# A two-layer decoder trunk: first pieces fetched first, norm squares on VectorE, matmuls in runs of two, three heads in flight

## The chip, the cores and the metric

The kernel runs on one core of a Trainium2 chip. A core has TensorE (matmuls; in the profile PE, with its weight loads as PEld), VectorE (DVE), ScalarE (ACT), GpSimd (POOL) and SyncE (SP, which here only issues transfers), an on-chip memory of 128 partitions (SBUF), and a small accumulator memory that matmuls write to (PSUM). Sixteen DMA engines move data from and to the chip's main memory. The metric is the device time of one execution in microseconds, as the median over several executions.

## The reference

Input x is 256 tokens of 2048 features, in float32. Two layers follow each other. Layer 0 mixes with a chunked gMLP (u, v) beside a gated linear recurrence, HGRN2 (q, f, i, g); layer 1 mixes with a forgetting attention of 16 heads. Each layer ends with a gated MLP that has a short convolution between its up-projection and its activation. Every part begins with an RMS norm and ends with a residual:

```python
def rms_norm(x, gain):
    xf = x.astype(jnp.float32)
    y = xf * lax.rsqrt(jnp.mean(xf * xf, axis=-1, keepdims=True) + RMS_EPS)
    return (y * gain.astype(jnp.float32)).astype(x.dtype)
...
for l in range(DEPTH):
    h = rms_norm(x, mix_norm[l])
    h = mixer_ab(h, ...) if l % 2 == 0 else mixer_c(h, ...)
    x = x + h
    h = rms_norm(x, ffn_norm[l])
    x = x + conv_ffn(h, ffn_w_up[l], ffn_conv_w[l], ffn_conv_b[l], ffn_w_down[l])
```

The projections hold nearly all of the arithmetic: six of 2048 x 1024 and one of 2048 x 2048 in layer 0's mixer, four of 2048 x 2048 (and a small one) and one of 2048 x 2048 in layer 1's, and in each MLP one of 2048 x 11264 and one of 5632 x 2048.

## The kernel before, in words

Features lie on partitions: x is held as 16 tiles (k-tiles) of 128 features by 256 tokens. A float32 product is made of three products of a narrower type: each operand is cut into a high part (a copy by ScalarE) and the rest (a subtraction by VectorE). `weights` (L129 to L142) does this for a chunk of weights: it has SP fetch the chunk into `w`, ScalarE make `wh` (L139) and VectorE `wl` (L141). The pool holds four `w` and three each of `wh` and `wl`; in the MLPs a second pool takes turns with it.

`project` (L144) makes one output tile of 128 features: 16 k-tiles (11 in the down projections) in two chunks. Each k-tile takes a pair of matmuls: `wh` against 512 columns, the high and the low part of the activations beside each other (L155), and `wl` against the 256 columns of the high part (L158). The argument `run` says how many `wh` matmuls stand in a row before their `wl` matmuls follow. Before the change it is 1 for f, q, g, u, w_cf and w_cg, 4 for w_abo and w_co, 2 for up and 3 for down in layer 0, 8 for up and 6 for down in layer 1.

`project_tok` (L164) makes tokens by features, 512 features at a time, for v, i and the attention's q, k, v. Each k-tile takes six matmuls 512 wide: L177, L178, L179 for each half of the tokens. For v's first half (`feed=True`) it also makes the activations on the way: `feed_split` scales a k-tile of x by the norm weights (columns of `pp`) and cuts it (L204, L205), and `feed_square` squares it on ScalarE (L240) and adds the squares into `acc` on GpSimd (L241). The first four chunks hold one k-tile, all others two.

The factor 1/rms is not in the activations: `norm.finish` gets it from `acc` with a matmul against ones and some small operations (`R`, and `Rt` for the token layout), and it is multiplied in after the projections. In v this is done by `finish`, a generator in a queue. `tick`, called once per chunk, advances up to `depth[0]` generators of the queue to their next `yield`; the recurrence's heads (`hgrn`), the gMLP's `mix` and the attention's heads run in the same way between the projections' chunks. A planner orders each engine's instructions from this program; every engine then takes its own in that fixed order.

At the start, GpSimd fetches the first 100 columns of `pp` (norm weights, hgrn gammas and other gains), SP the first piece of x, ScalarE the other four pieces, and TensorE runs 12 warm-up matmuls on a tile of ones. In layer 0's mixer ScalarE's queue later fetches the constants: `cst`, the gMLP's spatial weights `wt`, the rest of `pp`, and a mask.

`hgrn` (one generator per head) makes decay products at seven levels (`E`), their score matmuls (`smk`), adds them into `st`, and applies the result to i's tokens. `wt` and `E` share one tag of two buffers; `st` and `s128` have two buffers.

Of the kernel before, what the change touches and what calls it, by code (L numbers as in the profile page):

```python
# [7 lines left out]
F32 = mybir.dt.float32  # L8
# [6 lines left out]
P = 128  # L15
S = 256
D = 2048
KT = D // P
NH = 8
# [2 lines left out]
HT = HID // P  # L22
GRP = 11
EPS = 1e-6
WARM = 12
LEVELS = (64, 32, 16, 8, 4, 2, 1)
NL = len(LEVELS)
MCOLS = 2 * (NL + 1) * P
# [3 lines left out]
C_CW = 100  # L32
# [12 lines left out]
def tile_trunk(ctx: ExitStack, tc: tile.TileContext, x, pp_d, cst_d, mlev_d, msk_d,  # L45
# [13 lines left out]
    def nm(base):  # L59
        count[0] += 1  # L60
        return f"{base}_{count[0]}"

    xT = []
    xload = []
    for c0, n in ((0, 2), (2, 2), (4, 4), (8, 4), (12, 4)):
        t = cp.tile([P, n, S], F32, tag=f"x{c0}", name=f"x{c0}")
        xload.append((t, c0, n))
        xT += [t[:, i] for i in range(n)]
    pp = cp.tile([P, NPP], F32, tag="pp", name="pp")
    cst = cp.tile([P, NK], F32, tag="cst", name="cst")  # L70
    ones = cp.tile([P, P], F32, tag="ones", name="ones")
    one1 = cp.tile([P, 1], F32, tag="one1", name="one1")

    nc.gpsimd.dma_start(pp[:, 0:C_CW], pp_d[:, 0:C_CW])
    V.memset(ones, 1.0)
    V.memset(one1, 1.0)
    ident = cst[:, K_ID:K_ID + P]
# [37 lines left out]
    depth = [2]  # L115

    SC.preload_act_table_set(LNEXP)
    for i, (t, c0, n) in enumerate(xload):
        (SC if i else nc.sync).dma_start(t, x[:, c0:c0 + n, :])
    warm = pm.tile([P, 512], F32, tag="pm", name="warm")  # L120
    for i in range(WARM):
        PE.matmul(warm[:, 0:P], ones, ones, start=True, stop=True)
# [1 line left out]
    def drain():  # L124
        while flight or queue:
            tick()
# [14 lines left out]
        V.tensor_tensor(wl, w, wh.bitcast(F32), ALU.subtract)  # L141
        return wh, wl  # L142

    def project(wsrc, acts, chunks=(8, 8), k0=0, run=1):  # L144
        ps = pm.tile([P, 512], F32, tag="pm", name=nm("pm"))
        nk = sum(chunks)
        done = 0
        for c in chunks:
            lo = (k0 + done) * P
            tick()  # L150
            wh, wl = weights(wsrc[:, lo:lo + c * P], c * P)
            for k1 in range(0, c, run):
                ks = range(k1, min(k1 + run, c))
                for k in ks:
                    PE.matmul(ps, wh[:, k * P:(k + 1) * P], acts[done + k],  # L155
                              start=done + k == 0, stop=False, skip_group_check=True)
                for k in ks:
                    PE.matmul(ps[:, S:2 * S], wl[:, k * P:(k + 1) * P], acts[done + k][:, 0:S],  # L158
                              start=False, stop=done + k == nk - 1, skip_group_check=True)
            done += c  # L160
        return ps

    def project_tok(wsrc, norm, feed=False):
        ps = [pm.tile([P, 512], F32, tag="pm", name=nm("pm")) for _ in range(2)]  # L164
        k = 0
        for c in ((1, 1, 1, 1) + (2,) * 6 if feed else (2,) * 8):
            if feed:
                for i in range(c):
                    norm.feed_split(k + i)
            tick()  # L170
            wh, wl = weights(wsrc[:, k * 512:(k + c) * 512], c * 512)
            for T in range(2):
                for i in range(c):
                    a = norm.a[k + i]
                    ah, al = a[:, T * P:(T + 1) * P], a[:, S + T * P:S + (T + 1) * P]
                    h, l = (t[:, i * 512:(i + 1) * 512] for t in (wh, wl))
                    PE.matmul(ps[T], ah, h, start=k + i == 0, stop=False)  # L177
                    PE.matmul(ps[T], ah, l, start=False, stop=False)  # L178
                    PE.matmul(ps[T], al, h, start=False, stop=k + i == KT - 1)  # L179
            if feed:  # L180
                for i in range(c):
                    norm.feed_square(k + i, nc.gpsimd)
            k += c
        return ps

# [3 lines left out]
        V.tensor_tensor(t, ps[:, 0:S], t, ALU.add)  # L189
        return t  # L190

    def project_norm(wsrc, acts, R, out=None, run=1):
        t = fold(project(wsrc, acts, run=run))
        if out is None:
            out = t
        V.tensor_tensor(out, t, R, ALU.mult)  # L196
        return out
# [72 lines left out]
    def mixer_ab(norm):  # L270
# [10 lines left out]
        gv, late = [], []  # L281

        def finish():
            yield
            late.extend(norm.finish(tok=True))
            yield
            for T in range(2):
                act(gv[0][:, T], gv[0][:, T], AF.Gelu, scale=late[1][:, T:T + 1])
# [14 lines left out]
        A = norm.a  # L303

        SC.dma_start(cst, cst_d)
        wt = hp.tile([P, 2, NH, P], F32, tag="QK", name="wt", bufs=2)
        SC.dma_start(wt[:, 0], spw_d)
        SC.dma_start(wt[:, 1], spb_d.partition_broadcast(P))
        SC.dma_start(pp[:, C_CW:NPP], pp_d[:, C_CW:NPP])
# [63 lines left out]
        for h in range(NH):  # L373
# [9 lines left out]
            lf.append(l)  # L383
            kq.append(t)
        yB = [None] * KT

        itoks = []

        def hgrn(h):
            l, t = lf[h], kq[h]  # L390
            d0 = (h % 4) * P
            SC.activation(l, l, AF.Identity, bias=lb[:, h:h + 1], scale=omlb[:, h:h + 1])
            st = hp.tile([P, 2, P], F32, tag="st", name=nm("st"), bufs=2)
            dg = bank()
            for T in range(2):
                PE.matmul(dg[:, T * P:(T + 1) * P], t[:, T], t[:, 3 - T], start=True, stop=True)  # L396
# [2 lines left out]
            yield  # L399

            V.tensor_tensor(t[:, 2:4], t[:, 2:4], view(l, P, (-P, 2), (1, P)), ALU.mult)
            E = hp.tile([P, NL, 2, P], F32, tag="QK", name=nm("E"), bufs=2)
            tot = l
            for li in reversed(range(NL)):
                n = LEVELS[li]
# [17 lines left out]
            for c0, c1 in ((0, 4), (4, NL)):  # L423
                sps = bank()
                for li in range(c0, c1):
                    PE.matmul(sps[:, (li - c0) * P:(li - c0 + 1) * P],  # L426
                              E[:, li, 0], E[:, li, 1], start=True, stop=True)
                if c0 == 0:
                    xps = bank()
                    PE.matmul(xps[:, 0:P], t[:, 0], t[:, 2], start=True, stop=True)  # L430
                    s128 = hp.tile([P, P], F32, tag="s128", name=nm("s128"), bufs=2)
                    SC.activation(s128, xps[:, 0:P], AF.Copy)
                V.tensor_tensor(smk[:, c0 * P:c1 * P], sps[:, 0:(c1 - c0) * P],
                                msk[:, c0 * P:c1 * P], ALU.mult)
                for li in range(c0, c1):
                    n = LEVELS[li]
                    sv = view(st[:, 1], 0, (2 * n, 64 // n), (n - P, 2), (1, n))
                    V.tensor_tensor(sv, sv, smk[:, li * P:(li + 1) * P].rearrange(
                        "p (b two n) -> p b two n", two=2, n=n), ALU.add)
# [59 lines left out]
        for h in range(NH):  # L499
# [10 lines left out]
            if gates and not (queue or flight):  # L510
                queue.extend(spatial(b, z) for b, z in todo)
                todo = []
        drain()

        nxt = Norm(C_FFN)
        ks = [yB[8 + h] for h in range(NH)] + [yB[h] for h in range(NH)]
        for m in range(KT):
            add_x(m, project(w_abo[m], ks, run=4))
            nxt.feed(m)
        es.close()  # L520
        return nxt
# [2 lines left out]
    def mixer_c(norm):  # L524
# [109 lines left out]
            todo = []  # L634
        nxt = Norm(C_FFN + KT)
        for m in range(KT):
            add_x(m, project(w_co[m], yB, run=4))
            nxt.feed(m)
        es.close()
        return nxt  # L640
# [2 lines left out]
    def ffn(l, norm, last):  # L643
        es = ExitStack()
        hp = es.enter_context(tc.tile_pool(name="fp", bufs=1))
        deep.update(pool=es.enter_context(tc.tile_pool(name="fw", bufs=1)), turn=0)
        A = norm.a
        R = norm.finish()
        nxt = None if last else Norm(C_MIX + KT)

        def conv(j):
            z = project_norm(w_up[l, j], A, R, run=(2, 8)[l])

            def w(i):
                c = C_CW + (l * 3 + i) * 2 * HT + j
                return pp[:, c:c + 1]

            cb = C_CB + l * 2 * HT + j
            c = hp.tile([P, S], F32, tag="conv", name=nm("conv"), bufs=4)
            SC.activation(c, z, AF.Identity, bias=pp[:, cb:cb + 1], scale=w(2))  # L660
            V.scalar_tensor_tensor(c[:, 1:], z[:, :S - 1], w(1), c[:, 1:], ALU.mult, ALU.add)  # L661
            V.scalar_tensor_tensor(c[:, 2:], z[:, :S - 2], w(0), c[:, 2:], ALU.mult, ALU.add)  # L662
            return c

        def up(g):
            hid = []
            for i in range(GRP):
                j = g * GRP + i
                a = conv(j)
                b = conv(HT + j)  # L670
                act(a, a, AF.Silu)
                V.tensor_tensor(a, a, b, ALU.mult)
                t = hp.tile([P, 512], F32R, tag="hid", name=nm("hid"), bufs=2 * GRP)
                split(t, a)
                hid.append(t)
            return hid

        def down(g, hid):
            for m in range(KT):
                add_x(m, project(w_dn[l, m], hid, chunks=(6, 5), k0=g * GRP, run=(3, 6)[l]))  # L680
                if g == HT // GRP - 1:
                    if last:
                        nc.sync.dma_start(out[:, m, :], xT[m])
                    else:
                        nxt.feed(m)

        hids = [up(0)]
        for g in range(HT // GRP):
            if g + 1 < HT // GRP:
                hids.append(up(g + 1))  # L690
            down(g, hids[g])
        deep["pool"] = None
        es.close()
        return nxt
# [85 lines left out]
```

## Time and profile before

| | us |
|---|---|
| median of 3 runs (2371.09 to 2371.52) | 2371.42 |
| the profiled execution's own time | 2372.19 |
| its span, first to last instruction | 2370.4 |
| mean granted clock of TensorE over the span | 0.998 |
| TensorE busy | 2360.5 |
| VectorE busy | 1754.6 |
| ScalarE busy | 1324.8 |
| GpSimd busy | 16.2 |
| bytes read from main memory | 435.24 MB |

The profile is one execution. Its times count from the first instruction. A group or timeline line gives the line of the kernel, the engine, the operation, and the tiles as out<-in; in a timeline line the start and the duration stand first, and in brackets how long the engine was idle before and what ended that. A window line gives, for each engine, its busy time in that stretch and the number of instructions that touch it, then the granted clock of TensorE, the share of time that the DMA engines were busy, and GB/s. Matmuls overlap, so the duration of one is longer than its share of the time.

### The profile page before, as it was taken

The page shows a single profiled execution, that of the slowest core. Times are in us where ns is not written, and L with a number is a line of the kernel's source. Part 1 is how long each engine was busy: PE and PEld are TensorE (multiplying, and loading weights), DVE is VectorE, ACT ScalarE, POOL GpSimd, SP SyncE. Part 2 cuts the span into 40 slices and gives each one's busy share as a digit, 9 for nine tenths or more (in the row PEclk, how much of TensorE's full clock was granted, in tenths as well). Part 3 has the DMA queues.
Part 4 walks back from the last instruction along what each step waited for, and adds up shares of the span by engine and source line. Part 5 has one row for each costly group of instructions (what it writes and reads, how often), then busy time and mean ns, then how long its engine had stood idle before and what let it go on. Part 6 is the DMA issues. An engine that isn't in the chain of part 4 may idle for free.

```text
span 2370.4 us, 35641 instructions
## 1 busy us (share of the span) xinstructions
PE 2360.5 (100%) x13118; PEld 2045.7 (86%) x13118; DVE 1754.6 (74%) x2969; ACT 1324.8 (56%) x2249; POOL 16.2 (1%) x20
## 2 busy tenths in 40 slices
PE   9999999999999999999999999999999999999999
PEld 7888888888888888888888888888888888888888
DVE  7778886878767867867766666767778767767765
ACT  6655665655555555556555455556555555555543
POOL 2000000000000000000000000000000000000000
PEclk9999999999999999999999999999999999999999
DMA  7554455655575566566656554557555575575565
GB/s 259 178 167 153 152 190 202 223 191 190 156 211 198 167 193 206 172 174 187 198 170 182 171 161 167 187 189 238 194 187 187 155 223 189 153 222 189 153 190 145
DMA packets 133727, 439.69 MB, mean 185 GB/s; under 512 B 14865, under 2 KB 16929, under 8 KB 133425
## 3 DMA queue, kind: packets, MB, share of 16 engines
q1 hardware_dynamic: 132224, 433.40, 58.2%
q10 hardware_dynamic: 1296, 3.97, 0.5%
q8 instruction: 104, 1.70, 0.3%
q14 instruction: 71, 0.57, 0.1%
q0 software_dynamic: 32, 0.05, 0.0%
HBM read 435.24 MB, written 2.11 MB: 185 GB/s over the span
## 4 chain that ended last, share of the span: by engine, by line
PE 97%; DVE 2%; ACT 1%; issue 0%; DMA 0%; ACTq 0%; DVEq 0%; POOLq 0%
PE pm L155 53%; PE pm L158 27%; PE pm L178 5%; PE pm L177 5%; PE pm L179 5%; DVE wl L141 1%; PE px L426 1%; PE px L599 0%; PE px L563 0%; PE px L570 0%; DMA pp<-in_pp 0%; PE px L594 0%; DVE a L205 0%; PE px L396 0%; ACT wh L139 0%
## 5 line engine op out<-in xcount | busy, mean ns | idle before, releaser
L141 DVE TENSOR_TENSOR wl<-w,wh 128x1024 fp32r<-128x1024 f32 (+3 forms) x900 | 1015.8, 1129 | 519.2 <-ACT wh L139 513.4
L139 ACT ACTIVATE wh<-w 128x1024 fp32r<-128x1024 f32 (+3 forms) x900 | 883.2, 982 | 904.4 <-PE pm L155 635.1
L155 PE MATMUL pm<-a,wh 128*128 128x512 f32 x3600 | 1074.7, 395 | 0.0
L158 PE MATMUL pm<-a,wl 128*128 128x256 f32 x3600 | 694.5, 281 | 0.0
L155 PEld LDWEIGHTS pm<-a,wh 128*128 128x128 f32 x3600 | 614.9, 189 | 79.4 <-DVE a L205 0.8
L158 PEld LDWEIGHTS pm<-a,wl 128*128 128x128 f32 x3600 | 604.6, 189 | 76.5 <-issue 0.2
L155 PE MATMUL pm<-hid,wh 128*128 128x512 f32 x1408 | 389.0, 394 | 0.0
L155 PEld LDWEIGHTS pm<-hid,wh 128*128 128x128 f32 x1408 | 239.3, 189 | 27.9
L158 PEld LDWEIGHTS pm<-hid,wl 128*128 128x128 f32 x1408 | 219.8, 189 | 33.6
L158 PE MATMUL pm<-hid,wl 128*128 128x256 f32 x1408 | 228.9, 281 | 0.0
L177 PE MATMUL pm<-wh,a 128*128 128x512 f32 x512 | 203.8, 399 | 3.0 <-ACT wh L139 3.0
L178 PE MATMUL pm<-wl,a 128*128 128x512 f32 x512 | 201.9, 394 | 0.9 <-DVE wl L141 0.9
L179 PE MATMUL pm<-wh,a 128*128 128x512 f32 x512 | 201.1, 393 | 0.0
L177 PEld LDWEIGHTS pm<-wh,a 128*128 128x128 f32 x512 | 96.9, 189 | 22.5 <-ACT wh L139 3.2
L178 PEld LDWEIGHTS pm<-wl,a 128*128 128x128 f32 x512 | 96.9, 189 | 21.5 <-DVE wl L141 2.5
L179 PEld LDWEIGHTS pm<-wh,a 128*128 128x128 f32 x512 | 96.8, 189 | 20.0
L660 ACT ACTIVATE conv<-ev,pp 128x256 f32<-128x256 f32 x176 | 103.1, 586 | 18.2 <-DVE ev L196 18.1
L189 DVE TENSOR_TENSOR ev<-pm,ev 128x256 f32<-128x256 f32 x225 | 93.8, 417 | 4.2 <-ACT ev L188 4.2
L661 DVE SCALAR_TENSOR_TENSOR conv<-ev,pp,conv 128x255 f32<-128x255 f32 x176 | 84.2, 478 | 8.7 <-ACT conv L660 8.7
L662 DVE SCALAR_TENSOR_TENSOR conv<-ev,pp,conv 128x254 f32<-128x254 f32 x176 | 85.0, 483 | 6.2
L188 ACT ACTIVATE ev<-pm 128x256 f32<-128x256 f32 x225 | 82.5, 366 | 0.7 <-PE pm L158 0.6
L196 DVE TENSOR_TENSOR ev<-ev,R 128x256 f32<-128x256 f32 x184 | 78.2, 425 | 6.1
(176 smaller groups left out, 1453.5 us busy)
## 6 DMA issues: line engine op xcount, KB each, us to landing
w<-in_w_up SPq DMA_DIRECT2D x352, 512.0 KB, 4.2
w<-in_w_dn SPq DMA_DIRECT2D x128, 384.0 KB, 3.2
w<-in_w_cqkv SPq DMA_DIRECT2D x96, 512.0 KB, 3.7
w<-in_w_dn SPq DMA_DIRECT2D x128, 320.0 KB, 3.3
w<-in_w_abo SPq DMA_DIRECT2D x32, 512.0 KB, 3.5
w<-in_w_cg SPq DMA_DIRECT2D x32, 512.0 KB, 3.8
w<-in_w_co SPq DMA_DIRECT2D x32, 512.0 KB, 3.6
w<-in_w_f SPq DMA_DIRECT2D x16, 512.0 KB, 4.5
```

The source lines that it names most:

```text
L139: SC.activation(wh, w, AF.Copy)
L141: V.tensor_tensor(wl, w, wh.bitcast(F32), ALU.subtract)
L155: PE.matmul(ps, wh[:, k * P:(k + 1) * P], acts[done + k], start=done + k == 0, stop=False, skip_group_check=True)
L158: PE.matmul(ps[:, S:2 * S], wl[:, k * P:(k + 1) * P], acts[done + k][:, 0:S], start=False, stop=done + k == nk - 1, skip_group_check=True)
L177: PE.matmul(ps[T], ah, h, start=k + i == 0, stop=False)
L178: PE.matmul(ps[T], ah, l, start=False, stop=False)
L179: PE.matmul(ps[T], al, h, start=False, stop=k + i == KT - 1)
L188: SC.activation(t, ps[:, S:2 * S], AF.Copy)
L189: V.tensor_tensor(t, ps[:, 0:S], t, ALU.add)
L660: SC.activation(c, z, AF.Identity, bias=pp[:, cb:cb + 1], scale=w(2))
L661: V.scalar_tensor_tensor(c[:, 1:], z[:, :S - 1], w(1), c[:, 1:], ALU.mult, ALU.add)
L662: V.scalar_tensor_tensor(c[:, 2:], z[:, :S - 2], w(0), c[:, 2:], ALU.mult, ALU.add)
```

## The change

- `pp` is fetched in three parts: columns 0 to 31 (the norm weights of both mixers) first of all, by SP; columns 32 to 99 by ScalarE after `cst`; the convolution's as before.
- x comes in seven pieces instead of five. They are issued inside v's first four chunks (`FETCH`), the first eight k-tiles by SP between the chunks of w, the last eight by ScalarE. There are 15 warm-up matmuls instead of 12.
- The squares of the first norm leave v's first half: `finish` makes them during v's second half, three k-tiles per tick, and VectorE adds them.
- `run` is 2 in every `project`.
- `hgrn` has three heads in flight from the q and g projections to the end of u, with one `yield` more at its start, three buffers for `st` and `s128`, and a tag of its own for `E`; `wt` has one buffer.

```diff
-WARM = 12
+WARM = 15
+FETCH = {0: (0,), 1: (1, 2, 8), 2: (4, 6), 3: (12,)}
...
-    for c0, n in ((0, 2), (2, 2), (4, 4), (8, 4), (12, 4)):
+    for c0, n in ((0, 1), (1, 1), (2, 2), (4, 2), (6, 2), (8, 4), (12, 4)):
...
+    fetch = {c0: (t, c0, n) for t, c0, n in xload}
...
-    nc.gpsimd.dma_start(pp[:, 0:C_CW], pp_d[:, 0:C_CW])
+    nc.sync.dma_start(pp[:, 0:C_FFN], pp_d[:, 0:C_FFN])
...
-    for i, (t, c0, n) in enumerate(xload):
-        (SC if i else nc.sync).dma_start(t, x[:, c0:c0 + n, :])
...
-    def project(wsrc, acts, chunks=(8, 8), k0=0, run=1):
+    def project(wsrc, acts, chunks=(8, 8), k0=0, run=2):
...
             if feed:
+                for c0 in FETCH.get(k, ()):
+                    t, c0, n = fetch[c0]
+                    (SC if c0 >= 8 else nc.sync).dma_start(t, x[:, c0:c0 + n, :])
                 for i in range(c):
                     norm.feed_split(k + i)
...
-            if feed:
-                for i in range(c):
-                    norm.feed_square(k + i, nc.gpsimd)
             k += c
...
-    def project_norm(wsrc, acts, R, out=None, run=1):
+    def project_norm(wsrc, acts, R, out=None, run=2):
...
         def finish():
-            yield
+            for k in range(KT):
+                norm.feed_square(k)
+                if k % 3 == 2:
+                    yield
             late.extend(norm.finish(tok=True))
...
         SC.dma_start(cst, cst_d)
-        wt = hp.tile([P, 2, NH, P], F32, tag="QK", name="wt", bufs=2)
+        SC.dma_start(pp[:, C_FFN:C_CW], pp_d[:, C_FFN:C_CW])
+        wt = hp.tile([P, 2, NH, P], F32, tag="QK", name="wt", bufs=1)
...
+        depth[0] = 3
...
         def hgrn(h):
...
+            yield
             SC.activation(l, l, AF.Identity, bias=lb[:, h:h + 1], scale=omlb[:, h:h + 1])
-            st = hp.tile([P, 2, P], F32, tag="st", name=nm("st"), bufs=2)
+            st = hp.tile([P, 2, P], F32, tag="st", name=nm("st"), bufs=3)
...
-            E = hp.tile([P, NL, 2, P], F32, tag="QK", name=nm("E"), bufs=2)
+            E = hp.tile([P, NL, 2, P], F32, tag="E", name=nm("E"), bufs=2)
...
-                    s128 = hp.tile([P, P], F32, tag="s128", name=nm("s128"), bufs=2)
+                    s128 = hp.tile([P, P], F32, tag="s128", name=nm("s128"), bufs=3)
...
         drain()
+        depth[0] = 2
...
-            add_x(m, project(w_abo[m], ks, run=4))
+            add_x(m, project(w_abo[m], ks, run=2))
...
-            add_x(m, project(w_co[m], yB, run=4))
+            add_x(m, project(w_co[m], yB, run=2))
...
-            z = project_norm(w_up[l, j], A, R, run=(2, 8)[l])
+            z = project_norm(w_up[l, j], A, R, run=2)
...
-                add_x(m, project(w_dn[l, m], hid, chunks=(6, 5), k0=g * GRP, run=(3, 6)[l]))
+                add_x(m, project(w_dn[l, m], hid, chunks=(6, 5), k0=g * GRP, run=2))
```

## The prediction

> **What bounds the kernel now.** I read the page's first part and its chain of waits, then TensorE's time project by project, then the first 36 us.
>
> ```profile
> PE 2360.5 (100%) x13118; PEld 2045.7 (86%) x13118; DVE 1754.6 (74%) x2969; ACT 1324.8 (56%) x2249; POOL 16.2 (1%) x20
> ...
> PE 97%; DVE 2%; ACT 1%; issue 0%; DMA 0%; ACTq 0%; DVEq 0%; POOLq 0%
> ...
> L155 PE MATMUL pm<-a,wh 128*128 128x512 f32 x3600 | 1074.7, 395 | 0.0
> ```
>
> TensorE has work all the time and the chain lies on it for 97%. So an edit counts if it changes how fast matmuls follow each other, or fills TensorE's waits. The mean of 395 ns is no pace, for matmuls overlap. The pace comes from windows that begin and end with the start of a PSUM eviction, a whole number of projections apart:
>
> ```profile
> core 0: us, PE busy (x), PEclk, DMA share, GB/s
> 535.74:624.91 89.17, 89.17 (x514) 1.00 0.56 185
> 1756.81:1851.78 94.97, 94.97 (x546) 1.00 0.56 182
> 1024.54:1078.48 53.94, 53.94 (x310) 1.00 0.71 188
> 2308.49:2354.73 46.24, 46.24 (x266) 1.00 0.66 184
> 332.90:400.74 67.84, 67.84 (x386) 1.00 0.54 186
> 1549.29:1622.26 72.97, 72.97 (x418) 1.00 0.56 188
> 1481.13:1526.34 45.21, 45.21 (x258) 1.00 0.55 187
> ```
>
> In order: up of layer 0 (runs of 2), up of layer 1 (8), down of layer 0 (3), down of layer 1 (6), w_abo (4), w_co (4), w_cg (1). The count in brackets has two matmuls cut at the edges. An up, w_abo, w_co or w_cg projection has 16 pairs (one 512 wide on wh, one 256 wide on wl), a down projection 11. So one projection takes 89.17/16 = 5.573 us, 94.97/17 = 5.587, 53.94/14 = 3.853, 46.24/12 = 3.853, 67.84/12 = 5.653, 72.97/13 = 5.613, 45.21/8 = 5.651. Per pair: 348.3 ns in runs of 2, 349.2 in 8, 350.3 in 3 and 6, 353.3 and 350.8 in 4, 353.2 in 1. Runs of 1 also have a faster pattern: at the end of w_u the wh matmuls of the timeline start at 310.33, 310.68, 311.02 and 311.37, 347 ns apart. The order thus moves the pace by up to 2%, and one order can settle into more than one pattern.
>
> The start, from the timeline and from windows of all engines:
>
> ```profile
> 1.23 0.68 POOL L74 DMA_DIRECT2D pp<-in_pp  x1 [0.79 <-POOLq L769]
> ...
> 7.57 0.51 ACT L204 ACTIVATE a<-x,pp 128x256 fp32r<-128x256 f32 x1 [5.55 <-DMA pp<-in_pp]
> ...
> 8.65 1.22 PE L177 MATMUL pm<-wh,a 128*128 128x512 f32 x2 [3.01 <-ACT wh L139]
> ...
> 15.26 1.23 DVE L141 TENSOR_TENSOR wl<-w,wh 128x1024 fp32r<-128x1024 f32 x1 [0.15 <-ACT wh L139]
> ...
> 18.18 1.76 DVE L141 TENSOR_TENSOR wl<-w,wh 128x1024 fp32r<-128x1024 f32 x1
> ...
> 23.44 0.50 PE L178 MATMUL pm<-wl,a 128*128 128x512 f32 x1 [0.42 <-DVE wl L141]
> ```
>
> ```profile
> core 0: us, PE busy (x) PEld busy (x) DVE busy (x) ACT busy (x) POOL busy (x), PEclk, DMA share, GB/s
> 6.00:8.00 2.00, 0.00 (x0) 0.00 (x0) 0.36 (x3) 0.43 (x2) 0.00 (x0) 0.98 1.05 407
> 8.00:10.00 2.00, 1.35 (x3) 1.12 (x4) 1.95 (x7) 2.00 (x6) 0.00 (x0) 0.50 1.01 385
> 14.00:16.00 2.00, 2.00 (x9) 1.60 (x8) 1.84 (x3) 1.83 (x4) 0.75 (x2) 0.81 0.85 309
> ```
>
> The norm weights (pp) come last, at 7.55; the first matmul waits for them until 8.65. DMA is full from 4 to 14 us. The clock falls to 0.50 after the pause and comes back in the 14 to 16 us window. Beside GpSimd's adds a wl takes 1.76 us, not 1.23, and TensorE then waits for it.
>
> **Runs of 2.** They take as many matmuls as before; only the order changes. I price them at the 5.573 us that 88 projections of layer 0's up keep without one outlier past the second. Up of layer 1: 88 x (5.5865 - 5.5731) = 1.2 us. w_abo: 16 x 0.080 = 1.3. w_co: 16 x 0.040 = 0.6. w_cg: 16 x 0.078 = 1.2. Down: chunks of 6 and 5 give runs 2,2,2,2,2,1; five twos at 696.6 ns and a single at 350 (between 347 and 353) are 3.833 us against 3.853, and 128 x 0.020 = 2.6; bounds 0 (the two orders there already take equal time) and 3.0. The 32 projections of f, q, g and u go from 1 to 2: between 32 x (5.573 - 5.547) = 0.8 lost and 32 x 0.078 = 2.5 gained, by the two patterns; undisturbed pairs there average some 349.4 ns, so 512 x 1.1 = 0.5 gained. Up of layer 0 already has runs of 2: nothing. Sum 7.4 us gained, bounds 2.3 (down nothing, f to u 0.8 lost, w_cg and w_abo half) and 9.8.
>
> [...]
>
> **The start.** Before w's first chunk SP now issues pp and half as much x: 256 rows of partitions instead of 128. Before, x landed at 0.74 + 4.0 = 4.7 and w's first chunk at 1.18 + 5.2 = 6.4. If bytes count it lands by 6.4 again, if rows count 1.7 later, 8.1; I take 7.0, since both queues were sharing full DMA engines and rows got shorter. ScalarE's 0.61 us for wh then lets the first matmul go at 7.6 instead of 8.65. But all of x and the first four chunks of w are the same 3 MB. They were in at 11.8 before; now x pieces for later k-tiles stand ahead of w's second to fourth chunk on SP, and two 512 KB pieces share the engines from ScalarE's queue. So I expect those chunks 1 to 2 us later than before, and the fifth k-tile at 17.1 as before (17.07): after early work TensorE waits again. If the clock is lost in these pauses (matmuls started 427 ns apart from 9.67 on, so the six of a k-tile took 2.56 us, against 1.36 later), k-tiles two to four run from 10.9 and the fifth starts up to 1.8 later, at 18.9; if data comes by bytes it starts at 15, 2 earlier.
>
> [...]
>
> After the fifth k-tile the waits for wl go: k-tile starts 22.63 to 24.71 and 28.99 to 31.07 take 2.08 instead of 1.36 us, and smaller ones add 0.3: 1.75 gained, since GpSimd no longer adds. The squares' adds move to VectorE's second half of v: 15 x 0.42 (a 128x256 tensor-tensor) = 6.3 us over eight chunks, where it has 1.23 us of wl in each 2.72 of TensorE: hidden; with no cover 0.8 us a chunk. ScalarE's 16 squares of 0.40 move along, beside wh of 1.05 a chunk. R is done some 9 us later than before, but the norm's matmuls now stand behind five chunks of the second half, and f's first fold needs R only at its end. Behind VectorE's add stands the masking of wt, which waited 1.4 us for its DMA before; now a wl is queued behind it, and I charge 0.4 (bounds 0 and 1.4). The later columns of pp (hgrn's gammas among them) now travel behind cst on ScalarE's queue; their first reader stands in VectorE's queue in v's second half, three chunks behind the issue, and a chunk is 2.72 us where a landing took 4 to 6: nothing charged, and if they are late a wl is late behind them. The three more warm-up matmuls end about 6.1, ahead of any data. Together I take 1.0 us gained, bounds 4.5 gained and 2.5 lost.
>
> **Three heads in flight.** The same instructions. A head's q and g come every four ticks and a head takes ten (now eleven), so two in flight hold heads up a little; in the instruction order of the changed kernel the last heads' matmuls stand only half a projection earlier. From 106 to 315 us TensorE's loads waited 4 us in all for hgrn's operands; I take nothing, bounds half of these waits either way (2 gained, 2 lost). VectorE (167.65 us of 209 busy) hides the rest; where it can't, wl is late next.
>
> **Sum:** 7.4 + 1.0 + 0 = 8.4 us. The profiled execution took 2372.19 (span 2370.4 and 1.8 around it): 2363.8. The median of the runs lies 0.8 below that execution, so 2363.0.
>
> **Rivals.** [...] (b) The first pieces come by bytes and the clock holds: 3.5 more, 2359.5. For it DMA was full from 4 us and the first x needed only 4.0; against, ScalarE's order puts five splits ahead of the third wh. (c) The clock is lost and the start costs 2.0: 2366.0. For it, the clock at 0.50 in the 8 to 10 us window. (d) Slower: runs of 2 settle elsewhere into the 353.3 ns pattern that w_abo and w_cg show. Up of layer 1 then pays 1408 x 4.1 = 5.8, down 1408 x 3.0 = 4.2, w_co 256 x 2.5 = 0.6, f to u 512 x 3.9 = 2.0; with the start 11.6 lost, 2383.0. It decides from 350.4 ns a pair on: the 4,096 changed pairs now average 350.2, and the start gives 1.0 us over them. Against it, after the pause at 411 us runs of 2 came back to 5.574 within one projection.
>
> **Chances.** Forecast 0.55, (a) 0.12, (b) 0.15, (c) 0.10, (d) 0.08. The range goes from 2358.5 to 2369.5: it holds the forecast with the bounds of the runs and the start, (b) and (c), and leaves out (d), about half of (a) and the tails. With 0.2% (4.7 us, about what a measurement of this kernel tells from no change): faster 0.75, same 0.17 (mostly (a), part of (c)), slower 0.08.
>
> **What would show it.** Evictions 5.573 us apart in up of layer 1, w_abo, w_co and w_cg, and 3.83 in down: the runs' term. 3.85 in down takes 2.6 off; 5.65 anywhere is (d). First matmul near 7.6, fifth k-tile near 17.1, k-tiles 1.36 apart after it, wl at 1.23. A clock of 0.50 after 12 us is (c). A VectorE wait for wt's DMA with TensorE idle behind it would show the 0.4.

## The result and the profile after

| | before | after |
|---|---|---|
| median of the runs, us (7 each, side by side) | 2371.54 (2371.09 to 2372.52) | 2364.41 (2363.96 to 2364.58) |
| ratio of the medians | | 0.9969, 95% interval 0.9957 to 0.9981 |
| the profiled execution's own time, us | 2372.19 | 2364.58 |
| its span, us | 2370.4 | 2362.5 |

The changed kernel is 7.1 us faster; 8.4 were forecast. The page of the changed kernel, first part, chain of waits and the largest matmul group:

```profile
PE 2353.4 (100%) x13124; PEld 2034.5 (86%) x13124; DVE 1753.8 (74%) x2984; ACT 1324.2 (56%) x2249; POOL 0.2 (0%) x4
...
PE 99%; DMA 0%; ACT 0%; DVE 0%; SPq 0%; issue 0%; ACTq 0%
...
L155 PE MATMUL pm<-a,wh 128*128 128x512 f32 x3600 | 1135.3, 396 | 0.0
```

TensorE still sets the time, now for 99% of the chain. The group of L155 grew from 1074.7 to 1135.3 us although the kernel got faster. A group's busy time counts its own overlapping matmuls once, and in up of layer 1, where eight `wh` matmuls stood in a row and now two do, they cover one another less: 44 of its 88 projections hold 176.4 us of the group before and 221.0 after. A matmul group's busy time is therefore no price. The windows between evictions are, here of the changed kernel in the same order as before (up of layer 0, up of layer 1, down of both layers, w_abo, w_co, w_cg):

```profile
core 0: us, PE busy (x), PEclk, DMA share, GB/s
481.76:570.93 89.17, 89.17 (x514) 1.00 0.53 189
1751.37:1851.68 100.31, 100.31 (x578) 1.00 0.53 179
1024.52:1078.28 53.76, 53.76 (x311) 1.00 0.67 189
2301.27:2347.35 46.08, 46.08 (x267) 1.00 0.63 184
335.25:403.09 67.84, 67.84 (x386) 1.00 0.51 186
1549.82:1622.27 72.45, 72.45 (x418) 1.00 0.54 189
1482.88:1527.46 44.58, 44.58 (x258) 1.00 0.53 189
```

They hold 16, 18, 14, 12, 12, 13 and 8 projections. One takes 5.573 us in both ups, w_co and w_cg, and 3.840 in both downs. But w_abo takes 67.84/12 = 5.653, as before the change.

The start of the changed kernel, from the timeline (start, duration, engine, line, out<-in; in brackets the idle time before and what ended it) and from the windows of all engines:

```profile
0.73 0.38 SPq L76 DMA_DIRECT2D pp<-in_pp  x1
...
7.12 0.73 PE L180 MATMUL pm<-wh,a 128*128 128x512 f32 x2 [1.06 <-ACT wh L139]
...
9.57 0.50 PE L180 MATMUL pm<-wh,a 128*128 128x512 f32 x1 [0.52 <-ACT wh L139]
...
13.17 0.73 PE L180 MATMUL pm<-wh,a 128*128 128x512 f32 x2 [1.45 <-ACT wh L139]
...
16.30 0.63 PE L180 MATMUL pm<-wh,a 128*128 128x512 f32 x2
...
19.54 1.22 DVE L141 TENSOR_TENSOR wl<-w,wh 128x1024 fp32r<-128x1024 f32 x1
```

```profile
core 0: us, PE busy (x) PEld busy (x) DVE busy (x) ACT busy (x) POOL busy (x), PEclk, DMA share, GB/s
8.00:10.00 2.00, 1.48 (x5) 0.71 (x5) 0.70 (x2) 1.12 (x3) 0.00 (x0) 1.00 1.02 375
12.00:14.00 2.00, 0.83 (x3) 0.41 (x4) 1.25 (x3) 1.60 (x4) 0.00 (x0) 1.00 0.99 379
14.00:16.00 2.00, 2.00 (x9) 1.66 (x10) 1.81 (x4) 2.00 (x5) 0.00 (x0) 1.00 0.72 223
```

The first matmul comes at 7.12 instead of 8.65 us. TensorE then pauses several times for `wh`, at most 1.5 us long, and in this execution its clock stays at 1.00, where before it stood at 0.50 from 8 to 14 us. The fifth k-tile starts at 16.30 (17.07 before), the sixth at 18.39, and from there they are 1.36 us apart with `wl` at 1.22 to 1.23 us. The waits from 0 to 40 us of the changed kernel say the same (engine, line, what it waited for: us in total, times, longest):

```profile
PE pm L180 <- ACT wh L139: 3.0, 3, 1.5
...
PE pm L181 <- DVE wl L141: 0.7, 2, 0.4
...
DVE wt L318 <- DMA wt<-in_spw: 0.4, 1, 0.4
DVE gm L364 <- DMA pp<-in_pp: 0.4, 1, 0.4
```

VectorE's two waits for a transfer stop no matmul. To compare kernels I cut each profiled execution at the first matmul of each stage. The times of the stages in us (q, g is the stage of both, MLP the up and down of a layer):

| stage | before | after | difference |
|---|---|---|---|
| v (from 0) | 57.87 | 56.08 | -1.79 |
| f | 48.25 | 48.15 | -0.11 |
| q, g | 160.32 | 158.74 | -1.58 |
| u | 48.40 | 48.50 | +0.10 |
| w_abo | 90.82 | 90.66 | -0.16 |
| MLP of layer 0 | 737.72 | 736.87 | -0.85 |
| w_cf, attention's q, k, v | 295.85 | 295.67 | -0.17 |
| w_cg | 98.12 | 97.18 | -0.94 |
| w_co | 89.80 | 89.44 | -0.35 |
| MLP of layer 1 | 743.22 | 741.25 | -1.97 |

They sum to 7.8. The profiled execution of before lay 0.7 above the median of the runs, that of after 0.2, so the stages overstate the gain by some 0.5.

### The profile page after: what moved, and what is told of

The parts are those of the page before. It is cut to its first block, busy times and chain, and to the rows that moved or that the text cites. A ratio compares the mean times of both kernels' runs of the same rounds, so it can differ in the third digit from the quotient of the medians.

```text
span 2362.5 us, 35650 instructions
## 1 busy us (share of the span) xinstructions
PE 2353.4 (100%) x13124; PEld 2034.5 (86%) x13124; DVE 1753.8 (74%) x2984; ACT 1324.2 (56%) x2249; POOL 0.2 (0%) x4
## 4 chain that ended last, share of the span: by engine, by line
PE 99%; DMA 0%; ACT 0%; DVE 0%; SPq 0%; issue 0%; ACTq 0%
PE pm L155 54%; PE pm L158 27%; PE pm L182 5%; PE pm L181 5%; PE pm L180 5%; PE px L432 1%; DMA w<-in_w_v 0%; PE px L606 0%; PE px L570 0%; PE px L577 0%; PE px L601 0%; PE px L402 0%; PE px L339 0%; PE px L576 0%; PE px L607 0%; PE px L453 0%
## 5 line engine op out<-in xcount | busy, mean ns | idle before, releaser
L155 PE MATMUL pm<-a,wh 128*128 128x512 f32 x3600 | 1135.3, 396 | 0.0
L158 PEld LDWEIGHTS pm<-a,wl 128*128 128x128 f32 x3600 | 676.0, 188 | 158.9
L158 PE MATMUL pm<-a,wl 128*128 128x256 f32 x3600 | 708.6, 278 | 0.0
L155 PEld LDWEIGHTS pm<-a,wh 128*128 128x128 f32 x3600 | 549.4, 189 | 1.4 <-DVE a L205 0.8
L155 PE MATMUL pm<-hid,wh 128*128 128x512 f32 x1408 | 447.2, 395 | 0.0
L158 PEld LDWEIGHTS pm<-hid,wl 128*128 128x128 f32 x1408 | 264.6, 188 | 57.1
L158 PE MATMUL pm<-hid,wl 128*128 128x256 f32 x1408 | 287.9, 279 | 0.0
L155 PEld LDWEIGHTS pm<-hid,wh 128*128 128x128 f32 x1408 | 219.6, 189 | 5.2
```

What stands on the lines that cost most here:

```text
L155: PE.matmul(ps, wh[:, k * P:(k + 1) * P], acts[done + k], start=done + k == 0, stop=False, skip_group_check=True)
```

## The experiments

**The three parts, each alone.** Runs of 2 alone, on the kernel before:

```diff
-    def project(wsrc, acts, chunks=(8, 8), k0=0, run=1):
+    def project(wsrc, acts, chunks=(8, 8), k0=0, run=2):
...
-            add_x(m, project(w_abo[m], ks, run=4))
+            add_x(m, project(w_abo[m], ks, run=2))
...
-            z = project_norm(w_up[l, j], A, R, run=(2, 8)[l])
+            z = project_norm(w_up[l, j], A, R, run=2)
```

> The kernel before with runs of 2 in every projection and nothing else of the change. Theory (the three parts add up, each in its own stage): the stages behind u gain what they gain in the changed kernel, 4.3 us (layer 0's down 0.85, w_cg 0.94, w_co 0.35, layer 1's MLP 1.97, w_abo 0.16), v gains nothing (57.87 us stay), and the q and g stage gains at most the 0.5 us that I had put on f, q, g and u; in all 4.3 to 4.8. Rival (the 1.58 us of the q and g stage come from the order of the matmuls, not from three heads): the q and g stage falls by 1.6 here already, in all 5.9.

The start alone: the changed kernel with `run` and `hgrn` as before.

```diff
-    def project(wsrc, acts, chunks=(8, 8), k0=0, run=2):
+    def project(wsrc, acts, chunks=(8, 8), k0=0, run=1):
...
-        depth[0] = 3
```

> The changed kernel with the runs of before and two heads in flight: only the start and the norm's squares are changed. Theory: v takes 56.1 us instead of 57.87 (1.8 gained) and no later stage moves by more than 0.2; in all 1.8. Rival (the start only moves waits into f and q and g, where R is late): v gains 1.8 and f or q and g give back 0.5 or more.

Three heads alone, on the kernel before:

```diff
+        depth[0] = 3
...
         def hgrn(h):
...
+            yield
...
-            st = hp.tile([P, 2, P], F32, tag="st", name=nm("st"), bufs=2)
+            st = hp.tile([P, 2, P], F32, tag="st", name=nm("st"), bufs=3)
```

> The kernel before with three heads in flight (its extra yield, buffers and tag for E) and nothing else. Theory (three heads shorten the recurrence's waits): the q and g stage takes 158.7 us instead of 160.3, 1.6 gained, all others stay. Rival (the order of matmuls or the earlier start did it): q and g within 0.3 us of 160.3, in all 0.

| | median, us | before beside it less this | ratio, 95% interval |
|---|---|---|---|
| runs alone | 2366.52 | 4.6 | 0.9981, 0.9971 to 0.9990 |
| start alone | 2370.17 | 1.0 | 0.9996, 0.9987 to 1.0006 |
| heads alone | 2369.68 | 1.5 | 0.9993, 0.9984 to 1.0002 |

The runs are the largest part, so rival (a), order without effect, falls; the intervals of the other two include 1. The three gains add up to 7.1, but that is partly luck: the start alone and the heads alone both leave w_cg at `run=1`, and both show it fast, as this window of the start alone shows:

```profile
1491.34:1535.71 44.37, 44.37 (x258) 1.00 0.54 190
```

That is 44.37/8 = 5.546 us a projection. The kernel before had 5.651 there with the same order of the same matmuls at the same clock. So both profiled executions hold 1.2 us in w_cg that their part doesn't change; I go by the stages. The heads alone took 1.36 off q, g and put 0.74 on u.

In the profile of the start alone TensorE's clock fell, which it did not do in the profile of the changed kernel with the same start. Ahead of it stands a pause of 1.66 us. First the line of its timeline, then its windows for TensorE alone:

```profile
12.84 0.73 PE L180 MATMUL pm<-wh,a 128*128 128x512 f32 x2 [1.66 <-ACT wh L139]
```

```profile
14.00:16.00 2.00, 2.00 (x7) 0.55 0.87 256
16.00:18.00 2.00, 2.00 (x6) 0.60 0.89 352
```

That is 2 x (0.45 + 0.40) = 1.7 us of full clock lost. Its v took 56.59 us, 0.5 more than the changed kernel's. Three kernels further down have this start too: two heads, runs of 1 and the order table. All of them lost the clock there, after pauses of 1.82, 1.58 and 3.62 us, and their v took 56.87, 56.54 and 57.89 us.

**Two heads beside the rest.** The changed kernel with `hgrn` as before:

```diff
-        depth[0] = 3
...
-            yield
...
-            st = hp.tile([P, 2, P], F32, tag="st", name=nm("st"), bufs=3)
+            st = hp.tile([P, 2, P], F32, tag="st", name=nm("st"), bufs=2)
```

> The changed kernel with two heads in flight and the buffers of before. Theory (beside runs of 2 the third head is worth little): q and g and u together take 207.2 to 207.6 us, up to 0.4 more than the changed kernel's 207.2. Rival (the third head brings the 1.4 us that it brought q and g by itself): q and g take 160.1.

One run took 2365.46. Its q, g take 159.14 us (158.74 with three heads) and its u 48.27 (48.50): beside runs of 2 the third head is worth some 0.2 us. Runs alone took 1.17 off q, g. Most of the gain of that stage is the runs'.

**What order has what pace.** The changed kernel with another `run` in each group of the MLPs, and one small extra matmul (128 wide, its result unused) ahead of w_abo's projections 5 and 10 and ahead of some of layer 1's up, to see whether a pattern can be shifted:

```diff
+    RUN = ((1, 4, 8, 3), (1, 2, 4, 1))[l]
...
-            z = project_norm(w_up[l, j], A, R, run=2)
+            z = project_norm(w_up[l, j], A, R, run=RUN[g])
...
+            if m in (5, 10):
+                nudge()
             add_x(m, project(w_abo[m], ks, run=2))
```

> The changed kernel with other runs in the MLPs: up of layer 0 in groups with runs of 1, 4, 8, 3; up of layer 1 with 1, 2, 4, 1; down of layer 0 with 1, 2, 6, 4; down of layer 1 with 1, 3, 4, 2. One extra 128-wide matmul of ones in the middle of each group of layer 1's up and in front of the sixth and eleventh projection of w_abo. Theory (a pattern of starts locks in, and which one depends on where TensorE stands when it begins): w_abo leaves 5.653 us a projection for 5.573 after an extra matmul, and one order shows two paces in different groups (runs of 1: 5.547 and 5.65; runs of 4: 5.613 and 5.653). Rival (the operands of a stage set its pace): w_abo stays at 5.653 behind both extra matmuls, and an order has one pace in every up group.

It took 2373.91 us in one run. Windows of this kernel, TensorE alone: up of layer 0 in runs of 1, 4, 8 and 3, and up of layer 1 in runs of 1:

```profile
472.42:516.79 44.37, 44.37 (x259) 1.00 0.56 190
544.67:589.58 44.91, 44.91 (x258) 1.00 0.55 187
723.03:795.66 72.63, 72.63 (x418) 1.00 0.54 189
907.82:963.75 55.93, 55.93 (x323) 1.00 0.53 188
1694.20:1728.12 33.92, 33.92 (x194) 1.00 0.54 186
```

With 8, 8, 13, 10 and 6 projections these are 5.546, 5.614, 5.587, 5.593 and 5.653 us. Runs of 2 and 4 took the same pace in the ups of both layers, and so did runs of 8 (those of layer 1 before the change); runs of 1 have two paces within one execution. In down a projection took 3.813 in layer 0 and 3.887 in layer 1 with runs of 1, 3.840 with 2, and 3.853 with 3, 4 and 6. The extra matmul changed no pace in up. In w_abo the first of them changed nothing, and behind the second the projections went from 5.653 to 5.600.

**Runs of 1 in layer 0's MLP.** They can be the fastest order:

```diff
-            z = project_norm(w_up[l, j], A, R, run=2)
+            z = project_norm(w_up[l, j], A, R, run=(1, 2)[l])
...
-                add_x(m, project(w_dn[l, m], hid, chunks=(6, 5), k0=g * GRP, run=2))
+                add_x(m, project(w_dn[l, m], hid, chunks=(6, 5), k0=g * GRP, run=(1, 2)[l]))
```

> The changed kernel with runs of 1 in layer 0's up and down projections, 2 elsewhere. Theory (runs of 1 hold the faster of their two patterns there again): up at 5.547 and down at 3.813 us a projection, layer 0's MLP 88 x 0.026 + 64 x 0.027 = 4.0 us shorter than in the changed kernel, about 2360.4 in all. Rival (the slow pattern catches them in this program): up at 5.651 and down at 3.887, 88 x 0.078 + 64 x 0.047 = 9.9 longer, about 2374.

Ten runs fell into two groups: six from 2360.2 to 2362.0 and four from 2373.5 to 2374.9 us, with nothing between. The profiled execution was one of the second (span 2372.7), and its window in up of layer 0 has the slow pattern, 90.44/16 = 5.653:

```profile
482.63:573.07 90.44, 90.44 (x514) 1.00 0.56 187
```

From 5.653 to 5.547 for 88 projections and from 3.887 (this execution's down) to 3.813 for 64 are 9.3 + 4.7 = 14.0 us, about the distance of the groups (13). By this distance, for there is no trace of the faster group, one program lands in either pattern from one execution to the next. Runs of 2 give up the fast one and showed 5.573 in up in every profiled execution of this study.

**What the start gained from.** The changed kernel with the squares' adds back on GpSimd in v's first half:

```diff
             if feed:
                 for i in range(c):
                     norm.feed_split(k + i)
...
+            if feed:
+                for i in range(c):
+                    norm.feed_square(k + i, nc.gpsimd)
...
         def finish():
-            for k in range(KT):
-                norm.feed_square(k)
-                if k % 3 == 2:
-                    yield
+            yield
```

> The changed kernel, but with the squares added by GpSimd in v's first half again. Theory (the start's gain is that wl is no longer slowed by GpSimd): wl takes 1.7 us again beside GpSimd's adds, TensorE waits for it again in the first half, and v takes 57.3 to 57.9 us instead of 56.1. Rival (the gain is the earlier first pieces and the kept clock): v stays at 56.1 to 56.4.

One run took 2366.2, with v at 57.85 us, as in the kernel before. The first matmul still comes at 7.18. From the timeline of this kernel, one `wl` beside a GpSimd add and one without, and its waits of TensorE from 0 to 40 us:

```profile
18.18 1.76 DVE L141 TENSOR_TENSOR wl<-w,wh 128x1024 fp32r<-128x1024 f32 x1
...
25.09 1.21 DVE L141 TENSOR_TENSOR wl<-w,wh 128x1024 fp32r<-128x1024 f32 x1
```

```profile
PE pm L180 <- ACT wh L139: 2.3, 2, 1.9
PE pm L181 <- DVE wl L141: 1.8, 5, 0.5
```

Three profiles have the old start (before, runs alone, heads alone) and five the changed one without adds. From the start of the sixth k-tile to that of the seventeenth, the first of v's second half, the five take 14.96 to 14.98 us, this kernel 17.08 and the three 16.73 to 17.61. The adds are thus worth 1.8 to 2.6 us. The earlier first pieces alone give nothing: the sixth k-tile starts at 18.07 us here, at 18.39 to 20.22 in the five and at 17.12 to 18.43 in the three. TensorE begins 1.5 us sooner and then waits for chunks that come later. The Trainium skill's page SBUF — State Buffer, section SBUF: two separate sides, gives a reason for the slow `wl`: a VectorE operation with two SBUF inputs and a GpSimd one block each other, because they share a pair of ports. The 1.76 beside an add and 1.21 without agree with it; no run here separates ports from another cause.

**The norm weights by GpSimd.** In the changed kernel a transfer of x on SP waits 1.3 us before it is issued. Its waits of SP's queue from 0 to 15 us:

```profile
SPq L137 <- DVE wl L141: 3.5, 4, 1.4
SPq L137 <- DMA w<-in_w_v: 3.3, 3, 1.9
SPq L170 <- DMA x<-in_x: 1.3, 1, 1.3
```

That is the piece of k-tiles 6 and 7, issued at 5.34, just as the first piece landed (5.33). Its own tile was free. The third chunk of w likewise went at 6.44, as the first landed (6.42). So I took pp off SP's queue:

```diff
-    nc.sync.dma_start(pp[:, 0:C_FFN], pp_d[:, 0:C_FFN])
+    nc.gpsimd.dma_start(pp[:, 0:C_FFN], pp_d[:, 0:C_FFN])
```

> The changed kernel with the 32 columns of the norm weights fetched by GpSimd as before. Theory (the start is held by w's second to fourth chunk, not by the first matmul): the first matmul comes at about 8.6 us instead of 7.1 and v still takes 56.1 to 56.6. Rival (the first matmul's delay is passed on): v takes 57.6.

I expected the first matmul at 8.6, behind a late pp. It came at 7.18: pp's 32 columns landed at 6.08. One run took 2362.47, with v at 54.94, 1.1 less than in the changed kernel. The piece of k-tiles 6 and 7 was issued at 3.54 without a wait, and the third chunk of w landed at 10.16 instead of 12.46. TensorE's waits of this kernel from 0 to 40 us:

```profile
PE pm L180 <- ACT wh L139: 1.6, 2, 0.8
...
PE pm L181 <- DVE wl L141: 0.7, 2, 0.5
```

In this kernel w_abo, whose code is the changed kernel's, took 5.600 us a projection, 67.20/12:

```profile
333.95:401.15 67.20, 67.20 (x386) 1.00 0.56 188
```

**Runs of 8 in w_abo.** The kernel of the last experiment with

```diff
-            add_x(m, project(w_abo[m], ks, run=2))
+            add_x(m, project(w_abo[m], ks, run=8))
```

> The changed kernel with the norm weights fetched by GpSimd and runs of 8 in w_abo. Theory (with pp off the first eight transfers of the two queues, w's third and fourth chunk are issued earlier; and runs of 8 hold one pace): v takes 54.9 us instead of 56.1 to 56.9, w_abo 5.587 us a projection instead of 5.653, about 2362.2 in all. Rival (both were chance of one execution: w_abo has two patterns whatever its order, and v varies by a microsecond): v between 56 and 57, w_abo at 5.65, 2364.4.

The median is 2363.64 (ratio 0.9967, 0.9955 to 0.9979), with v at 54.81 us, but w_abo at 5.653. Runs of 8 do not help there; w_abo showed 5.653 with runs of 2, 4 and 8 and 5.600 with 2, and the windows of both at a clock of 1.00.

**x in the order of need.** In addition all of x on SP, each piece ahead of the chunk that needs it, and none on ScalarE's queue:

```diff
-FETCH = {0: (0,), 1: (1, 2, 8), 2: (4, 6), 3: (12,)}
+FETCH = {0: (0,), 1: (1, 2), 2: (4,), 3: (6,), 6: (8,), 8: (12,)}
...
-                    (SC if c0 >= 8 else nc.sync).dma_start(t, x[:, c0:c0 + n, :])
+                    nc.sync.dma_start(t, x[:, c0:c0 + n, :])
```

> As the run with norm weights by GpSimd and runs of 8 in w_abo, and x's last eight k-tiles are issued by SP behind the first five chunks of w, in the order in which they are needed. Theory (the start is held by the landing of w's second to fourth chunk, which share the engines with x pieces that are needed later): w's fourth chunk lands 2 to 3 us earlier, the fifth k-tile starts at 13 us instead of 15, v takes 52.5 to 53.5 us, 2360.5 in all. Rival (ScalarE's queue sets the start, with splits, conversions and squares): v stays at 54.5 to 55.

The fifth k-tile starts at 13.37 instead of 14.83, but v takes 56.72 and the median is 2364.39. The timeline of this kernel shows a part of where it went:

```profile
20.24 0.17 DVE L364 TENSOR_TENSOR gm<-pp 128x8 f32<-128x8 f32 x1 [1.39 <-DMA pp<-in_pp]
...
20.52 1.22 DVE L141 TENSOR_TENSOR wl<-w,wh 128x1024 fp32r<-128x1024 f32 x1
...
21.80 0.50 PE L181 MATMUL pm<-wl,a 128*128 128x512 f32 x1 [1.80 <-DVE wl L141]
```

VectorE stands 1.39 us at `gm`, a small operation on 8 columns of hgrn's gammas, until the late part of pp has landed. Behind it in VectorE's order stands a `wl`, and TensorE waits 1.80 us for that. The prediction had named this hazard (the late columns make a `wl` late) and charged nothing. After this pause the clock fell as well, as the windows of TensorE alone show:

```profile
22.00:24.00 2.00, 2.00 (x7) 0.72 0.70 211
24.00:26.00 2.00, 2.00 (x6) 0.50 0.72 211
26.00:28.00 2.00, 2.00 (x9) 0.92 0.90 315
```

They hold 2 x (0.28 + 0.50 + 0.08) = 1.7 us of full clock lost. Not every run seems to lose it: three of the eight, this profile's among them, took 2365.56 to 2366.00 us at a mean clock of 0.999, the other five 2363.59 to 2364.86 at 1.000.

**More warm-up or less.** The kernel with runs of 8 in w_abo, with

```diff
-WARM = 15
+WARM = 12
```

> As the run with norm weights by GpSimd and runs of 8 in w_abo, with 12 warm-up matmuls as before. Theory (pauses of under 2 us keep the clock): the granted clock stays at 1.00 after 4 us and v stays at 54.9. Rival (three more warm-up matmuls are what keeps it): the clock falls to 0.50 around 8 us as before the change, and v takes 1 to 2 us more.

The median is 2363.6, v 54.81, the clock 1.00 throughout: the three extra matmuls did nothing here. TensorE's longest pause behind the first matmul was 0.53 us; whether they matter in the changed kernel, with its longer pauses, was not tried.

**x in order, and pp in one piece.** As x in order, but pp's first 100 columns in GpSimd's one transfer, as before the change, and w_abo in runs of 2:

```diff
-    nc.gpsimd.dma_start(pp[:, 0:C_FFN], pp_d[:, 0:C_FFN])
+    nc.gpsimd.dma_start(pp[:, 0:C_CW], pp_d[:, 0:C_CW])
...
-        SC.dma_start(pp[:, C_FFN:C_CW], pp_d[:, C_FFN:C_CW])
```

> The kernel with x in the order of need on SP, with one thing changed back: all 100 first columns of pp come in GpSimd's one transfer, as in the kernel before (and w_abo goes back to runs of 2). Theory: with x in order the fifth k-tile started at 13.4 instead of 14.8, and that gain was lost only because VectorE's gm waited 1.4 us for pp's columns 32 to 99 with a wl queued behind it. Those columns now have no transfer of their own, so the wait for pp ahead of gm is gone, the k-tile starts from the sixth on are 1.36 apart, and v takes 52.5 to 53.5; the median is near 2362. Rival: the wait only shows where another one would end last, namely that splits and wl of the sixth to eighth chunk come late from VectorE and ScalarE whatever pp does; then TensorE still waits some 2 us for wl between 18 and 26 us, v is 54.5 or more, and the time is 2363.5 or more. A second rival: GpSimd's larger transfer lands later (7.5 as in the kernel before, not 6.1) and the first matmul starts at 8.6 instead of 7.2, which takes the gain back.

The median is 2361.89 us (2361.66 to 2362.46; ratio to before 0.9959, 0.9945 to 0.9973), and v takes 53.69, 0.2 above the range that the theory gave. This kernel's waits of TensorE from 0 to 40 us, without the warm-up's:

```profile
PE pm L181 <- DVE wl L141: 0.7, 3, 0.3
```

In its first 20 us TensorE is busy for 18.12 us, in the changed kernel for 15.27. First a line of the windows of this kernel, then the same of the changed kernel:

```profile
0.00:20.00 20.00, 18.12 (x79) 1.00 0.89 320
```

```profile
0.00:20.00 20.00, 15.27 (x68) 1.00 0.84 286
```

pp landed at 4.67, `gm` ran at 4.69 as VectorE's first work on data, and the first matmul came at 6.58. No wait for pp stands ahead of a `wl` any more, TensorE's longest pause behind the first matmul is 0.33 us, and its clock stays at 1.00. This version beats both kernels: 2361.89 against 2364.41 and 2371.54.

## Why the prediction was right, and where it was not

The sign, the size and the likeliest case were right: the orders set the pace, and TensorE's time fell. Term by term, by the stages:

- **Runs, 7.4 forecast, some 5.7 measured.** Up of layer 1 gave 88 x (5.587 - 5.573) = 1.2, as forecast. w_cg gave 0.94 (1.2) and w_co 0.35 (0.6): their first projections, beside the norm or the attention's rest, gained less than the settled ones that I had measured. The 0.94 hangs on the execution: w_cg in runs of 1 took 98.12 us in the profile of before but 96.90 with the start alone and with the heads alone, less than the 97.18 in runs of 2. Down gave 128 x (3.853 - 3.840) = 1.7 (2.6): evictions alternate 3.83 and 3.85 apart, and I had priced every projection by the first. f, q, g and u gave some 1.4 (0.5), by the runs alone: 0.11 + 1.17 + 0.13.
- **The step that failed is w_abo: 1.3 forecast, 0.16 measured.** I took its 5.653 for the pace of runs of 4 and 5.573 for what runs of 2 would do. The same page showed w_co at 5.613 with the same runs of 4, and that difference was the sign that w_abo's pattern isn't set by the run's length. It kept 5.653 with runs of 2, 4 and 8, and 5.600 came and went with nothing changed in it. Rival (d), runs of 2 in a 353.3 ns pattern, thus came true in this stage alone. Why w_abo differs from w_co stays open: of two extra matmuls in it one moved it, the other did not.
- **The start, 1.0 forecast, 1.8 measured in the profile.** The first matmul (7.6 forecast) came at 7.12 and the fifth k-tile (17.1) at 16.30; but the sixth came at 18.39, against 18.43 before, so nothing was left of the earlier pieces. What gained was the 1.75 for the waits behind the slow `wl`, as forecast (the kernel with the adds back takes 2.1 more there); the squares on VectorE hid, as forecast. The 0.4 charged for the mask of wt did not come: VectorE waited 0.4 us, TensorE not. The 1.8 is also luck of two executions: v took 57.43 to 57.87 us in the three profiles with the old start and 56.08 to 57.89 in the five with the changed one, by their means 0.8 less.
- **The clock.** In the profile of the changed kernel rival (c) did not come: 1.00 throughout, with pauses up to 1.5 us. But in the other four profiles with this start the clock fell after 12 us, which the prediction had named as the sign of (c), for 1.7 us of full clock each. The pause ahead of it was 1.66 us in the start alone, 1.58 in runs of 1, 1.82 in two heads and 3.62 in the order table. The old start lost it after 3.01 us in before and after 2.36 in the heads alone, and kept it after 1.83 in the runs alone. The Trainium skill, "TensorE: Matmul & The Clock Gate", section Why this matters for your kernels, has the clock fall after idle gaps over some 3 us. The profiles of before and after agree with that; the falls after 1.58, 1.66, 1.82, 2.36 and, with x in order, 1.80 us do not. As 1.83 us, and 1.94 with the adds on GpSimd, kept the clock, a pause's length alone does not decide; what does stays open.
- **Rival (b), the start by 4.5 us,** did not come in the changed kernel, but it was there to be had: x in order with pp in one piece takes 57.87 - 53.69 = 4.2 off v. What stood between was what the prediction left out: pp on SP's queue delayed a piece of x and the third chunk of w until earlier transfers had landed, and ScalarE's large pieces of x, not needed yet, shared the DMA engines.
- **Three heads, 0 forecast, 0.2 measured** beside runs of 2.

Sum: 5.7 + 1.8 + 0.2 = 7.7, against 7.8 by the stages. That the terms add up holds for this pair of profiles; between executions of the same orders v alone moved by up to 1.8 us and w_cg by 1.2.

## What to carry to other kernels

Price an order of matmuls by windows a whole number of outputs long, in several stages and, where the same order shows two paces, in several executions: such an order has two patterns, and its better one can't be counted on. At a start that waits for data, count the transfers that are in flight ahead of the one that is needed next; a small one on the busy queue can delay a large one by more than it takes itself. Ask of every small operation that waits for a transfer what stands behind it on its engine: 8 columns of gammas cost 1.8 us of TensorE here, and the clock after that. Look at the granted clock of a start in more than one execution: one profile that keeps it does not show that the next will.

## What was not expected of the hardware

- Runs of 1 (one 512-wide matmul, one 256-wide) have two stable patterns, 5.547/16 = 346.7 and 5.653/16 = 353.3 ns a pair, at a granted clock of 1.00 in both. The same orders took one or the other from execution to execution (w_cg at 5.651 and 5.546 us a projection; 13 us between the two groups of runs) and from stage to stage. w_abo has two as well, 5.600/16 = 350.0 and 353.3 ns.
- An issue can wait, with its own tile free, for the landing of a transfer that went seven or eight places ahead of it over SP's and ScalarE's queues: 5.34 after a landing at 5.33, 6.44 after 6.42. With pp fetched by GpSimd the first of these waits was gone. The trace's records show what is waited for: the transfers of both queues signal their landing on eight semaphores by turns, and the two issues wait for the one that they will signal themselves (numbers 102 and 103), last taken by the first piece of x and the first chunk of w. A transfer on GpSimd's queue takes none of the eight.
- pp's 32 columns by GpSimd landed at 6.08 us and its 100 columns at 4.67, once no x came from ScalarE's queue (its 32 columns then at 4.24): what else is in flight weighed more than the transfer's own size.
- The clock of one and the same start held in one execution and fell to about half in four, after pauses of TensorE as short as 1.58 us; each fall cost 1.7 us of full clock. A longer pause, 1.94 us, kept it elsewhere.
